# Gate and up products of a split-precision SwiGLU: heads and rests of the tokens in one 512-column matmul

## The chip, the cores and the metric

The kernel runs on one core of one Trainium2 chip. The metric is the device time in microseconds. The kernel before takes 1000.98 us, the median of three runs (1000.97 to 1001.18). All profile rows come from one profiled execution on that core.

## The reference

A trunk of two residual layers over 512 tokens of width 1024, in float32. Layer 0 mixes tokens by causal pooling, layer 1 by dilated window attention. Each layer ends with the block that the change touches:

```python
def swiglu(h, w_gate, w_up, w_down):
    g = jnp.einsum('bsd,df->bsf', h, w_gate)
    u = jnp.einsum('bsd,df->bsf', h, w_up)
    return jnp.einsum('bsf,fd->bsd', jax.nn.silu(g) * u, w_down)

for i in range(DEPTH):            # DEPTH = 2
    h = rmsnorm(x, norm_mix[i])
    x = x + (pool_mixer(h, ...) if i % 2 == 0 else attn_mixer(h, ...))
    h = rmsnorm(x, norm_ffn[i])
    x = x + swiglu(h, w_gate[i], w_up[i], w_down[i])
return rmsnorm(x, norm_final)
```

The hidden width of this block is 2816, which is 22 tiles of 128.

## The kernel before, in words

**Precision.** Every float32 operand is split into a head in the fp32r type and a rest, also fp32r. A product is then three matmuls that accumulate in one PSUM region: weight head by token head, weight head by token rest, weight rest by token head. ACT casts the head (line 139 for weights, line 320 for other tiles) and DVE subtracts it to get the rest (lines 143 and 321).

**Seven products in place of eight.** In groups of two hidden tiles, gate and up are computed by a two-by-two scheme of the Strassen kind: the inner width is cut into halves, the tokens into halves of 256, and sums of weight blocks meet sums of token blocks in seven products, numbered 0 to 6. The token operands (`RIGHT`) are blocks of the normalised tokens `h` or sums of such blocks (`t2`, `t3`, `t4`). The weight sums are made by accumulating DMAs (line 107, on POOL's queue) and by DVE sums (line 145). There are eleven groups per layer, two weight tiles (gate and up) by four inner tiles in each product, so a product has 8 x 3 = 24 matmuls of 256 columns (line 625), each with its own weight load. Seven products use three accumulators, p, r and q: product 0 starts p, 1 starts r, 3 starts q, and 2, 4, 5, 6 add to p or r (`"prpqprp"`). After each product ACT or DVE copies or combines the accumulator into the tile `ct` (`done`, lines 632 to 661); after products 5 and 6 come silu, the gating products, and the sums and splits that make the operands `u_hi` and `u_lo` of the down projection.

**Down.** After groups 3, 6 and 9 a down step (`down`, line 696) multiplies the gated results of three groups by the down weights, again in seven products, each 18 matmuls of 512 columns (line 712) in two token blocks; DVE adds each accumulator into the residual `x` (lines 719 and 721). The last two groups have a plain form (lines 766 to 768).

**Order.** PE runs in the order of the program text; the other engines are ordered by priorities (`URGENT` for accumulator copies after products 0 to 4). Within the feed-forward block, PE's order is `FFN_ORDER`: groups 0 and 1 interleaved, then group by group, each down step as a whole after its group. The weights stand in one queue in the same order. `weights(i)` loads up to ten entries ahead into five raw tiles (`wraw`; three more, `vraw`, for sums), and splits up to four ahead into a ring of five head and rest tiles (`RING`, `wspl`): entry k takes the buffers of entry k - 5. `held` counts entries that an earlier position in the queue still occupies.

**PSUM.** There are eight banks of 512 float32 columns. Four are the rotating pool `mm`, four the feed-forward block's pool `fps` (two for p, two for r). An accumulator of a group is half gate, half up, 256 columns each, in one bank.

Four lines of the product:

```python
for g in range(2):
    for c in range(4):
        for k, (w, xx) in enumerate(((whi, hi), (whi, lo), (wlo, hi))):
            nc.tensor.matmul(ps[:, g, :], lhsT=w[:, g, c, :], rhs=xx[:, c, :], ...)
```

Of the kernel before, what the change touches and what calls it, by code (L numbers as in the profile page):

```python
# [10 lines left out]
F32 = mybir.dt.float32  # L11
# [35 lines left out]
FFN_ORDER = (  # L47
    [("two", 0)] + [("quad", n) for n in (2, 3)] + [("down", 0)]
    + [("quad", n) for n in (4, 5, 6)] + [("down", 1)] + [("quad", n) for n in (7, 8, 9)] + [("down", 2)]
    + [("quad", 10)] + [("last", 3)]  # L50
)

TWO = [(g, i) for g in (0, 1) for i in (0, 3)] + [(g, i) for i in (1, 2, 4, 5, 6) for g in (0, 1)]
# [5 lines left out]
def trunk_kernel(ctx: ExitStack, tc: tile.TileContext, x_in, xT, gam, gains, consts, ident_d, w0, wT, w1, wv, w_down, out):  # L59
# [15 lines left out]
    mm = ctx.enter_context(tc.tile_pool(name="mm", bufs=4, space=bass.MemoryType.PSUM))  # L75
# [92 lines left out]
    def enqueue_ffn(layer):  # L168
# [27 lines left out]
        def down(b):  # L196
            pairs = BLOCKS[b]
            at = layer * (NF // 2) + pairs[0]
            dn[b] = [{}, {}]
            for i in range(7):  # L200
                for js, a, n in zip(dn[b], (at, at + 2), (2, len(pairs) - 2)):
                    operand(js, i, lambda m, k: tiles[k, :, a : a + n, COLS[m]], (n, S), 10)

        for step, n in FFN_ORDER:
            if step == "two":
                for g, i in TWO:
                    quad(n + g, i, 5)
            elif step == "quad":
                for i in range(7):
# [32 lines left out]
    h_both = [stat.tile([P, NC * S + 2 * SHIFT], F32R, name=f"h_{part}") for part in ("hi", "lo")]  # L242

    def tokens_at(shift):
        return [h[:, shift : shift + NC * S].rearrange("p (c s) -> p c s", c=NC) for h in h_both]
# [105 lines left out]
    def out_projection(js, where, hi, lo, norm, shift, four, tps, hook=None):  # L351
# [22 lines left out]
        ws = [weights(js[4 + i], split_ahead=4 + i, load_ahead=6 + i) for i in range(4)]  # L374
        for b in range(4):
# [20 lines left out]
    with ExitStack() as pctx:  # L396
# [137 lines left out]

        third = out_projection(j_out, BY_GROUP, z_hi, z_lo, norm, SHIFT, [mm.tile([P, S], F32, name="mm") for _ in range(4)], turned_banks, lambda: group_products(1, early))

    def ffn(layer, norm, third, nxt):
# [8 lines left out]
        with ExitStack() as fctx:  # L546
# [5 lines left out]
            fps = open_pool("ffps", 2, space=bass.MemoryType.PSUM)  # L552
            early_u = open_pool("ffa", 2)
            third_chain = norm.chain.ins
            h_hi, h_lo = tokens_at(SHIFT)
            block = lambda t, k, n: t[:, 4 * k : 4 * k + 4, HALVES[n]]

# [3 lines left out]
            t2, t3, t4 = ([fp.tile([P, 4, 256], F32R, name=f"t_{part}{i}") for part in ("hi", "lo")] for i in (2, 3, 4))  # L561
            fp.tile([P, SHIFT], F32, name="gap3")
            T_hi, T_lo = ([block(h, 0, 1), t2[i], t3[i], t4[i]] for i, h in enumerate((h_hi, h_lo)))
            RIGHT = (
                [(block(h_hi, 0, 0), block(h_lo, 0, 0))] + [(T_hi[i], T_lo[i]) for i in (0, 1)]
                + [(block(h_hi, 1, 0), block(h_lo, 1, 0)), (T_hi[2], T_lo[2])]
                + [(block(h_hi, 1, 1), block(h_lo, 1, 1)), (T_hi[3], T_lo[3])]
            )
# [12 lines left out]
            class Group:  # L581


                def __init__(self, n, ct):
                    self.n, self.ct, self.sums = n, ct, {}
                    self.lst = ct.rearrange("p m n g c -> p (m n g) c")
                    pool = early_u if n % 4 < 2 else late_u[0]
                    self.u = u_of[n] = [pool.tile([P, 7, 256], F32R, name=t) for t in ("u_hi", "u_lo")]

                def first_half(self):  # L590

                    (hi, lo), lst = self.u, self.lst
# [21 lines left out]
                def product(self, i):  # L614
                    if i == 3:
                        self.sums["q"] = mm.tile([P, S], F32, name="mm").rearrange("p (g c) -> p g c", g=2)
                    elif i < 2:
                        self.sums["pr"[i]] = fps.tile([P, 2, 256], F32, name="pr"[i])
                    ps = self.sums["prpqprp"[i]]
                    whi, wlo = weights(gu[self.n][i])  # L620
                    hi, lo = RIGHT[i]
                    for g in range(2):
                        for c in range(4):
                            for k, (w, xx) in enumerate(((whi, hi), (whi, lo), (wlo, hi))):
                                nc.tensor.matmul(  # L625
                                    ps[:, g, :], lhsT=w[:, g, c, :], rhs=xx[:, c, :],
                                    start=i in (0, 1, 3) and g + c + k == 0, stop=c == 3 and k == 2, skip_group_check=True,
                                )
                    with tc.high_priority(URGENT if i < 5 else 100):
                        self.done(i)  # L630

                def done(self, i):
# [12 lines left out]
                    elif i == 5:  # L645
                        nc.vector.tensor_add(ct[:, 0, 1], r, ct[:, 0, 1])
                        nc.scalar.activation(ct[:, 0, :, 0, :], ct[:, 0, :, 0, :], AF.Silu)
                        nc.vector.tensor_mul(ct[:, 0, :, 0, :], ct[:, 0, :, 0, :], ct[:, 0, :, 1, :])
                        nc.scalar.activation(ct[:, 1, 1, 0, :], ct[:, 1, 1, 0, :], AF.Silu)
                        nc.vector.tensor_mul(ct[:, 1, 1, 0, :], ct[:, 1, 1, 0, :], ct[:, 1, 1, 1, :])  # L650
                        self.first_half()
# [42 lines left out]
            r_tile = lambda: by_four(fps.tile([P, 2, 256], F32, name="r").rearrange("p g c -> p (g c)"))  # L694

            def down(b):

                pairs = BLOCKS[b]

                p, r = ([fps.tile([P, 2, 256], F32, name=t).rearrange("p g c -> p (g c)") for _ in range(2)] for t in "rp")  # L700
                q = [mm.tile([P, S], F32, name="mm") for _ in range(2)]
                where = (0, 1, 2, 3, 6, 5, 4)
                target = ((0, 0, 1), (1, 1, -1), (0, 1, 1), (0, 0, 1), (1, 1, -1), (0, 1, 1), (1, 0, -1))
                for i, acc in enumerate((p, r, p, q, p, r, p)):
                    ws = [weights(js[i], held=z) for z, js in enumerate(dn[b])]
                    half, n, sign = target[i]
                    for t in range(2):
                        for c, pair in enumerate(pairs):
                            whi, wlo = (w[:, c % 2, :] for w in ws[c // 2])
                            hi, lo = (u[:, where[i], t * P : (t + 1) * P] for u in u_of[pair])  # L710
                            for k, (u, w) in enumerate(((hi, whi), (hi, wlo), (lo, whi))):
                                nc.tensor.matmul(  # L712
                                    acc[t], lhsT=u, rhs=w, start=i in (0, 1, 3) and c + k == 0,
# [3 lines left out]
                        with tc.high_priority(URGENT):  # L717
                            if sign > 0:
                                nc.vector.tensor_add(to, acc[t], to)
                            else:  # L720
                                nc.vector.tensor_sub(to, to, acc[t])

            for kind, n in FFN_ORDER[:-1]:
                if kind == "two":
                    groups = [Group(n, ct_common), Group(n + 1, ct_tile(hn, "ct_second"))]
                    with tc.issue_after(third_chain):
                        first_tokens(0, t1r)
                        first_tokens(1, b21r)
                    for at, (g, i) in enumerate(TWO):
                        if at in (0, 2):  # L730
                            b = 2 + at // 2
                            if b == 2:
                                late_banks[b] = third
# [513 lines left out]
```

## Time and profile before

| what | value |
|---|---|
| median of the runs | 1000.98 us |
| profiled execution, first to last instruction (span) | 998.8 us |
| PE busy | 990.8 us, 6575 matmuls |
| PE weight loads busy | 908.1 us |
| DVE busy | 784.4 us |
| ACT busy | 529.1 us |
| granted TensorE clock, mean | 0.999 |

The profile gives no other time for its execution than the span; what lies around it, the median less the span, is 2.2 us. Busy time is the union of an engine's instructions. PE's matmuls overlap in their tails, so a matmul's duration (281 ns for 256 columns) is longer than the distance from one start to the next. Weight loads are listed as PEld and run beside the matmuls. A row of a group reads: line, engine, operation, tiles written and read, shapes, count, then total busy time, mean duration, and the idle time of the engine before them with what ended it. A row of the timeline begins with start and duration.

### The profile page before, as it was taken

How to read it: one execution, taken by the hardware profiler on the slowest of the kernel's cores; microseconds unless marked ns; L12 is line 12 of the kernel's file. 1: busy time of each engine (PE TensorE's matmuls, PEld its weight loads, DVE VectorE, ACT ScalarE, POOL GpSimd, SP SyncE). 2: the span in 40 equal slices, each digit the busy share in tenths (PEclk: the TensorE clock that was granted, in tenths of full speed). 3: DMA queues.
4: the chain of work that ended last, by engine and by line, in shares of the span. 5: the costliest groups of instructions: out<-in, count | busy, mean ns of one | idle time of the engine just before them, and what ended most of it. 6: DMA issues, size and time to landing. Idle time of an engine off the chain costs nothing.

```text
span 998.8 us, 16590 instructions
## 1 busy us (share of the span) xinstructions
PE 990.8 (99%) x6575; PEld 908.1 (91%) x6575; DVE 784.4 (79%) x1116; ACT 529.1 (53%) x838; POOL 113.1 (11%) x114
## 2 busy tenths in 40 slices
PE   9999999999999999999999999999999999999997
PEld 8888999989989998989888899899998998999896
DVE  6475899898888888777887457479989889788875
ACT  5573666545644554573543544356654554455354
POOL 0002010110111100002112023101011101211000
PEclk9999999999999999999999999999999999999999
DMA  9457276668559755524211249527666855975522
GB/s 335 177 168 190 63 197 174 152 189 234 149 128 290 179 137 155 182 71 134 85 56 53 83 141 267 103 61 191 179 159 198 235 148 121 294 176 141 153 66 84
DMA packets 76461, 157.29 MB, mean 157 GB/s; under 512 B 5904, under 2 KB 6288, under 8 KB 76384
## 3 DMA queue, kind: packets, MB, share of 16 engines
q1 hardware_dynamic: 58000, 121.00, 36.2%
q0 software_dynamic: 18096, 34.98, 20.5%
q8 instruction: 51, 0.84, 0.3%
q10 hardware_dynamic: 288, 0.27, 0.1%
q14 instruction: 26, 0.21, 0.1%
HBM read 154.08 MB, written 2.13 MB: 156 GB/s over the span
## 4 chain that ended last, share of the span: by engine, by line
PE 98%; ACT 1%; DVE 0%; issue 0%; ACTq 0%
PE p L625 25%; PE r L625 13%; PE r L712 10%; PE mm L625 6%; PE p L712 5%; PE mm L766 4%; PE mm L227 4%; PE mm L229 4%; PE mm L228 4%; PE mm L712 2%; PE early L443 2%; PE mm L363 2%; PE mm L361 2%; PE mm L362 2%; PE mm L1129 1%; PE tp L955 1%
## 5 line engine op out<-in xcount | busy, mean ns | idle before, releaser
L139 ACT CAST whi<-wraw 128x1024 fp32r<-128x1024 f32 (+2 forms) x189 | 184.8, 981 | 184.3 <-issue 50.8
L143 DVE TENSOR_TENSOR wlo<-wraw,whi 128x1024 fp32r<-128x1024 f32 (+2 forms) x190 | 221.1, 1165 | 74.8 <-ACT whi L139 74.1
L139 ACT CAST whi<-vraw 128x1024 fp32r<-128x1024 f32 (+1 forms) x102 | 99.6, 976 | 144.8 <-DVE vraw L145 53.7
L625 PE MATMUL p<-t_hi,wlo 128*128 128x256 f32 x528 | 149.8, 284 | 0.0
L625 PE MATMUL p<-t_lo,whi 128*128 128x256 f32 x528 | 149.4, 283 | 0.0
L625 PE MATMUL p<-t_hi,whi 128*128 128x256 f32 x528 | 148.4, 281 | 0.0
L143 DVE TENSOR_TENSOR wlo<-vraw,whi 128x1024 fp32r<-128x1024 f32 (+1 forms) x102 | 114.9, 1127 | 13.9 <-ACT whi L139 13.7
L625 PEld LDWEIGHTS p<-t_hi,whi 128*128 128x128 f32 x528 | 100.0, 189 | 0.0
L625 PE MATMUL r<-h_hi,wlo 128*128 128x256 f32 x352 | 99.9, 284 | 0.0
L625 PEld LDWEIGHTS p<-t_hi,wlo 128*128 128x128 f32 x528 | 99.6, 189 | 0.0
L625 PE MATMUL r<-h_lo,whi 128*128 128x256 f32 x352 | 99.6, 283 | 0.0
L625 PEld LDWEIGHTS p<-t_lo,whi 128*128 128x128 f32 x528 | 99.3, 188 | 0.0
L625 PE MATMUL r<-h_hi,whi 128*128 128x256 f32 x352 | 99.0, 281 | 0.0
L145 DVE TENSOR_TENSOR vraw<-vraw,wraw 128x1024 f32<-128x1024 f32 x68 | 76.6, 1127 | 0.8
L107 POOL DMA_DIRECT2D wraw<-w x22 | 26.6, 1211 | 436.1 <-DVE wlo L143 126.2
L625 PEld LDWEIGHTS r<-h_hi,whi 128*128 128x128 f32 x352 | 66.7, 189 | 0.0
L625 PEld LDWEIGHTS r<-h_hi,wlo 128*128 128x128 f32 x352 | 66.4, 189 | 0.0
L625 PEld LDWEIGHTS r<-h_lo,whi 128*128 128x128 f32 x352 | 66.2, 188 | 0.0
L227 PE MATMUL mm<-h_hi,whi 128*128 128x512 f32 (+1 forms) x176 | 64.9, 369 | 0.0
L229 PE MATMUL mm<-h_hi,wlo 128*128 128x512 f32 (+1 forms) x176 | 63.6, 361 | 0.0
L228 PE MATMUL mm<-h_lo,whi 128*128 128x512 f32 (+1 forms) x176 | 63.4, 360 | 0.0
L712 PE MATMUL r<-whi,u_lo 128*128 128x512 f32 x144 | 56.1, 390 | 0.0
(329 smaller groups left out, 2493.2 us busy)
## 6 DMA issues: line engine op xcount, KB each, us to landing
wraw<-w SPq DMA_DIRECT2D x116, 512.0 KB, 4.9
wraw<-w_down SPq DMA_DIRECT2D x32, 512.0 KB, 3.6
vraw<-w SPq DMA_DIRECT2D x22, 512.0 KB, 5.5
wraw<-w POOLq DMA_DIRECT2D x22, 512.0 KB, 7.6
vraw<-w POOLq DMA_DIRECT2D x22, 512.0 KB, 9.0
wraw<-wT SPq DMA_DIRECT2D x16, 512.0 KB, 4.4
wraw<-w_down SPq DMA_DIRECT2D x24, 256.0 KB, 2.6
vraw<-w_down SPq DMA_DIRECT2D x6, 512.0 KB, 5.4
```

The costliest lines, as they stand in the source:

```text
L107: nc.gpsimd.dma_start(dst, more, accum_op=ALU.add)
L139: nc.scalar.copy(hi[:, :n], raw[:, :n])
L143: nc.vector.tensor_sub(lo[:, :n], raw[:, :n], hi[:, :n].bitcast(F32))
L145: nc.vector.tensor_add(raws[into][:, :n], raws[into][:, :n], raws[more][:, :n])
L227: nc.tensor.matmul(ps, lhsT=whi, rhs=xhi, start=first, stop=False, **kw)
L228: nc.tensor.matmul(ps, lhsT=whi, rhs=xlo, start=False, stop=False, **kw)
L229: nc.tensor.matmul(ps, lhsT=wlo, rhs=xhi, start=False, stop=last, **kw)
L361: nc.tensor.matmul(ps, lhsT=xhi, rhs=w[0][:, k, :], start=first, stop=False)
L362: nc.tensor.matmul(ps, lhsT=xhi, rhs=w[1][:, k, :], start=False, stop=False)
L625: nc.tensor.matmul(ps[:, g, :], lhsT=w[:, g, c, :], rhs=xx[:, c, :], start=i in (0, 1, 3) and g + c + k == 0, stop=c == 3 and k == 2, skip ...
L712: nc.tensor.matmul(acc[t], lhsT=u, rhs=w, start=i in (0, 1, 3) and c + k == 0, stop=c == len(pairs) - 1 and k == 2, skip_group_check=True,)
L766: nc.tensor.matmul(ps, lhsT=u, rhs=w[:, m, :], start=z + m + k == 0, stop=z == 1 and m == 1 and k == 2,)
```

## The change

In groups 2 to 9 of each layer (`PAIRED`) a triple of matmuls becomes a pair for products 0, 2, 3, 5 and 6. The token tiles for heads and rests are made as one tile with an extra index z, so one matmul moves the 256 head columns and the 256 rest columns under the weight head, into the two halves of a bank: results with heads go to the first half, results with rests to the second. The weight rest by token head follows as a 256-column matmul into the first half. Products 1 and 4 keep three matmuls of 256 columns, product 1 into a second half, product 4 into a first.

A bank now holds one weight tile, so an accumulator is a pair of banks. A group has three: a (which alternates between two pairs from group to group), q and c. Product 0 starts a, which ACT copies whole into q; product 2 adds to a, and ACT copies a whole into c. Product 3 adds to q, 1 and 5 to c, 4 and 6 to a. When a result leaves its pair, ACT copies the second half into `ct` and DVE adds the first half.

PE's order is written out (`PLAN`): within a group 2, 3, 1, 4, then product 0 of the next group, then 5 and 6. In the queue the weights of 1, 2, 3, 4 stand in that order. Where a down step falls, its product 0 comes ahead of the group's 5 and 6, its products 1 to 5 after them, then the next group's product 0, then its product 6. The down step's accumulators are the free bank pair, q's pair and c's pair. The pool `mm` becomes one tile of four banks, handed out in turn by `Ring`. The tiles `u` are opened when first written.

```diff
-FFN_ORDER = (
-    [("two", 0)] + [("quad", n) for n in (2, 3)] + [("down", 0)]
...
+BODY, USED = (1, 2, 3, 4), (2, 3, 1, 4)
+PAIRED = range(2, 10)
+
+
+def _plan():
+    first = lambda n: [("quad", n, 0)] if n in PAIRED else []
+    steps = TWO[:-1] + first(2) + TWO[-1:]
+    for n in PAIRED:
+        steps += [("quad", n, i) for i in USED]
+        ends = [("quad", n, 5), ("quad", n, 6)]
+        if n % 3 == 0:
+            b = n // 3 - 1
+            steps += [("down", b, 0)] + ends + [("down", b, i) for i in range(1, 6)] + first(n + 1) + [("down", b, 6)]
+        else:
+            steps += first(n + 1) + ends
+    return steps + [("one", 10, i) for i in range(7)] + [("last", 3, 0)]
...
-    mm = ctx.enter_context(tc.tile_pool(name="mm", bufs=4, space=bass.MemoryType.PSUM))
+    mm_banks = ctx.enter_context(tc.tile_pool(name="mm", bufs=1, space=bass.MemoryType.PSUM)).tile([P, 4, S], F32, name="mm")
...
+    mm = Ring(*(mm_banks[:, i, :] for i in range(4)))
...
-        for step, n in FFN_ORDER:
...
+        for kind, n, i in PLAN:
+            if kind == "one":
+                quad(n, i, 5 if n < 2 else 10)
+            elif kind == "quad":
+                if i == USED[0]:
+                    for each in BODY:
+                        quad(n, each)
+                elif i not in BODY:
                     quad(n, i)
-            elif step == "down":
-                down(n)
+            elif kind == "down":
+                down(n, i)
...
-    h_both = [stat.tile([P, NC * S + 2 * SHIFT], F32R, name=f"h_{part}") for part in ("hi", "lo")]
+    h_both = stat.tile([P, 2, NC * S + 2 * SHIFT], F32R, name="h")
...
+            F0, F1 = (fps.tile([P, 2, S], F32, name=f"f{i}") for i in range(2))
+            M0, M1 = mm_banks[:, 0:2, :], mm_banks[:, 2:4, :]
...
-                def product(self, i):
+                def product(self, i, held=0):
+                    whi, wlo = weights(gu[self.n][i], held=held)
+                    right = RIGHT[i]
+                    if self.pairs:
+                        a, q, c = self.pairs
+                        to = (a, c, a, q, a, c, a)[i]
+                        for g in range(2):
+                            for k in range(4):
+                                w, rest, more = whi[:, g, k, :], wlo[:, g, k, :], dict(skip_group_check=True)
+                                if i in (1, 4):
+                                    at = to[:, g, HALVES[i == 1]]
+                                    nc.tensor.matmul(at, lhsT=w, rhs=right[:, 0, k, :], start=False, stop=False, **more)
+                                    nc.tensor.matmul(at, lhsT=w, rhs=right[:, 1, k, :], start=False, stop=False, **more)
+                                else:
+                                    at = to[:, g, HALVES[0]]
+                                    both = to[:, g, :].rearrange("p (z c) -> p z c", z=2)
+                                    nc.tensor.matmul(both, lhsT=w, rhs=right[:, :, k, :], start=i == 0 and k == 0, stop=False, **more)
+                                nc.tensor.matmul(at, lhsT=rest, rhs=right[:, 0, k, :], start=False, stop=k == 3, **more)
+                        with tc.high_priority(URGENT if i < 5 else 100):
+                            self.paired_done(i)
+                        return
...
+                def paired_done(self, i):
+                    ct = self.ct
+                    a, q, c = self.pairs
+                    own, more = HALVES
+                    if i == 0:
+                        nc.scalar.copy(q, a)
+                    elif i == 2:
+                        nc.scalar.copy(c, a)
+                    elif i == 3:
+                        nc.scalar.copy(ct[:, 0, 0], q[:, :, more])
+                        nc.vector.tensor_add(ct[:, 0, 0], q[:, :, own], ct[:, 0, 0])
+                    elif i == 1:
+                        nc.scalar.copy(ct[:, 1, 1], c[:, :, more])
+                    elif i == 4:
+                        nc.vector.scalar_tensor_tensor(
+                            ct[:, 1, 1], a[:, :, own], -1.0, ct[:, 1, 1], op0=ALU.mult, op1=ALU.subtract
+                        )
+                    elif i == 5:
+                        nc.scalar.copy(ct[:, 0, 1], c[:, :, more])
+                        nc.vector.tensor_add(ct[:, 0, 1], c[:, :, own], ct[:, 0, 1])
+                        self.gate_first()
+                    elif i == 6:
+                        nc.scalar.copy(ct[:, 1, 0], a[:, :, more])
+                        nc.vector.scalar_tensor_tensor(
+                            ct[:, 1, 0], a[:, :, own], -1.0, ct[:, 1, 0], op0=ALU.mult, op1=ALU.subtract
+                        )
+                        nc.scalar.activation(ct[:, 1, 0, 0, :], ct[:, 1, 0, 0, :], AF.Silu)
+                        nc.vector.tensor_mul(ct[:, 1, 0, 0, :], ct[:, 1, 0, 0, :], ct[:, 1, 0, 1, :])
+                        self.second_half()
...
+                if kind == "down":
+                    if i == 0:
+                        downs[n] = Down(n, spare_pairs[0], M0, F1)
+                        spare_pairs.reverse()
+                    downs[n].product(i)
+                    continue
+                if i == 0 and kind == "quad":
+                    groups[n] = Group(n, ct_common, (spare_pairs[0], M0, F1))
+                    spare_pairs.reverse()
+                elif n == 10 and i == 0:
+                    groups[n] = Group(n, ct_common)
+                groups[n].product(i, held={1: -2, 2: 1, 3: 1}.get(i, 0) if kind == "quad" else 0)
```

`gate_first`, not shown, holds the silu and gating lines of product 5 that stood in `done`; `Down` holds the matmuls and sums of `down`, one product per call.

More of the change, by code (lines that the diff above doesn't have):

```diff
@@ L615, in product @@
                     if i == 3:
[L616 removed]
+                        self.sums["q"] = by_g(mm.tile())
                     elif i < 2:
[L618 removed]
+                        self.sums["pr"[i]] = by_g((fp_ring, fr_ring)[i].tile())
                     ps = self.sums["prpqprp"[i]]
[L620 removed]
@@ L693, in ffn, with __init__, product @@
             by_four = lambda t: t.rearrange("p (j t) -> p j t", j=4)
[L694 to L705, printed above, removed]
+            r_tile = lambda: by_four(fr_ring.tile())
+            class Down:
+                def __init__(self, b, p, r, q):
+                    self.b, self.accs = b, (p, r, p, q, p, r, p)
+                def product(self, i):
+                    pairs, js = BLOCKS[self.b], dn[self.b]
+                    where = (0, 1, 2, 3, 6, 5, 4)
+                    target = ((0, 0, 1), (1, 1, -1), (0, 1, 1), (0, 0, 1), (1, 1, -1), (0, 1, 1), (1, 0, -1))
+                    ws = [weights(j[i], held=z) for z, j in enumerate(js)]
                     half, n, sign = target[i]
                     for t in range(2):
+                        acc = self.accs[i][:, t, :]
                         for c, pair in enumerate(pairs):
@@ L718, in down @@
                             if sign > 0:
-                                nc.vector.tensor_add(to, acc[t], to)
+                                nc.vector.tensor_add(to, acc, to)
                             else:
[L721 to L733, printed above, removed]
-                                norm.prepare(3, COLS)
-                            else:
-                                late_banks[b] = [r_tile(), by_four(mm.tile([P, S], F32, name="mm"))]
-                                for half in range(2):
-                                    norm.turn(b, half, late_banks[b][half])
-                            late(b, 1)
-                        if at in (4, 6, 8):
-                            for b in (2, 3):
-                                late(b, at // 2)
-                        groups[g].product(i)
@@ new lines, in product @@
+                                nc.vector.tensor_sub(to, to, acc)
+            mm.at = 0
+            groups = {0: Group(0, ct_common), 1: Group(1, ct_tile(hn, "ct_second"))}
+            downs, spare_pairs = {}, [M1, F0]
+            with tc.issue_after(third_chain):
+                first_tokens(0, t1r)
+                first_tokens(1, b21r)
+            for at, (kind, n, i) in enumerate(PLAN[:-1]):
+                if at in (0, 2):
+                    b = 2 + at // 2
+                    if b == 2:
+                        late_banks[b] = third
+                        norm.prepare(3, COLS)
+                    else:
+                        late_banks[b] = [r_tile(), by_four(mm_banks[:, 3, :])]
+                        for half in range(2):
+                            norm.turn(b, half, late_banks[b][half])
+                    late(b, 1)
+                if at in (4, 6, 8):
+                    for b in (2, 3):
+                        late(b, at // 2)
+                if kind == "down":
[10 more added lines that the diff above has]
+                groups[n].product(i, held={1: -2, 2: 1, 3: 1}.get(i, 0) if kind == "quad" else 0)
+                if (n, i) == (1, 6):
@@ L744, in ffn @@
                     held.close()
                     late_u.append(open_pool("ffb", 2))
-                elif kind == "quad":
-                    group = Group(n, ct_common)
-                    for i in range(7):
-                        group.product(i)
-                else:
-                    down(n)
             norm = Norm(nxt, ct_common.rearrange("p m n g c -> p (m n g c)")[:, :D])
```

80 lines of the change are left out of this document (43 added, 37 removed).

## The prediction

> **What bounds the kernel now.** I began with the shares by engine and the chain of waits on the page, then went to PE's own waits.
>
> ```profile
> span 998.8 us, 16590 instructions
> PE 990.8 (99%) x6575; PEld 908.1 (91%) x6575; DVE 784.4 (79%) x1116; ACT 529.1 (53%) x838; POOL 113.1 (11%) x114
> ...
> PE 98%; ACT 1%; DVE 0%; issue 0%; ACTq 0%
> PE p L625 25%; PE r L625 13%; PE r L712 10%; PE mm L625 6%; PE p L712 5%; PE mm L766 4%; PE mm L227 4%; PE mm L229 4%; PE mm L228 4%; PE mm L712 2%; PE early L443 2%; PE mm L363 2%; PE mm L361 2%; PE mm L362 2%; PE mm L1129 1%; PE tp L955 1%
> ```
>
> ```profile
> PE mm L261 <- DVE odd_rows L255: 1.1, 1, 1.1
> PE mm L1129 <- ACT ropea L1115: 0.3, 1, 0.3
> ```
>
> PE is the chain, and it waits 1.4 us in all. L625, the gate and up products, holds 44% of the span. So time is won only by shortening PE's stream, and lost as soon as something makes PE wait. The span lies 2.2 us under the median of 1000.98; I keep those 2.2 us and add to the median.
>
> A busy PE tells nothing of its pace, so I counted starts in stretches with one kind of matmul. First two rows of the groups by shape, for the duration of one (281 and 389 ns), then the stretches: length, PE busy (count), PEld, DVE, ACT, POOL, clock, DMA share, GB/s.
>
> ```profile
> L625 PE MATMUL p<-t_hi,whi 128*128 128x256 f32 x528 | 148.4, 281 | 0.0
> ...
> L712 PE MATMUL r<-whi,u_hi 128*128 128x512 f32 x144 | 56.0, 389 | 0.0
> ```
>
> ```profile
> 158.00:194.00 36.00, 36.00 (x306) 36.00 (x305) 31.61 (x37) 20.92 (x28) 4.48 (x4) 1.00 0.67 161
> 226.00:282.00 56.00, 56.00 (x469) 56.00 (x469) 45.43 (x52) 31.42 (x41) 6.91 (x6) 1.00 0.74 190
> ...
> 375.00:400.00 25.00, 25.00 (x112) 20.70 (x111) 21.62 (x29) 10.32 (x14) 2.00 (x2) 1.00 0.60 160
> ...
> 448.00:452.30 4.30, 4.30 (x38) 4.30 (x37) 4.01 (x9) 3.25 (x7) 0.60 (x1) 1.00 0.76 232
> 201.00:209.40 8.40, 8.40 (x38) 6.94 (x37) 8.40 (x11) 4.35 (x5) 0.00 (x0) 1.00 0.16 38
> ```
>
> A count takes in the matmuls cut by the edges, so the duration of one goes on top of the stretch. Groups 4 to 6 (second row): (56.00 + 0.28) / 469 = 120.0 ns from one 256-column matmul to the next. Groups 2 and 3 (first row): 36.28 / 306 = 118.6 ns, from the same code. The down products of 512 columns (third row): (25.00 + 0.39) / 112 = 226.7 ns. Twice the columns cost 106.7 ns more, so 120.0 - 106.7 = 13.3 ns of each pair of weight load and matmul do not depend on columns. The clock is 1.00 in all these rows.
>
> **The change, part by part.**
>
> *Fewer pairs on PE.* In groups 2 to 9 of both layers, products 0, 2, 3, 5 and 6 issue for each of 8 weight tiles (gate/up by 4) one 512-column and one 256-column matmul in place of three of 256. That is 16 x 5 x 8 = 640 triples, each one load and one matmul fewer, with the same columns. A triple goes from 360.0 to 226.7 + 120.0 = 346.7 ns: 13.3 ns saved in groups 4 to 9, 355.8 - 346.7 = 9.1 in groups 2 and 3. Of the 640, 480 are of the first kind and 160 of the second: 6.4 + 1.5 = **7.8 us off PE's stream**. The trace has no alternation of the two sizes. If the 118.6 rhythm comes back after the change in the 1,408 narrow matmuls left in those groups (640 in triples, 768 in products 1 and 4), up to 1,408 x 1.4 = 2.0 us more are saved; if every triple starts from 118.6, 640 x 9.1 = 5.8. I take 7.8 with 5.8 to 9.8 as ends. A wide product then takes 8 x 346.7 = 2.77 us, a narrow one 24 x 120.0 = 2.88, a group 19.6 in place of 20.2.
>
> The wide matmul reads its columns in two runs, from the heads and from the rests. The nearest row is the fourth above: there the by-halves projection (L227 to L229) reads and writes 256 columns in four runs of 64, at (4.30 + 0.28) / 38 = 120.5 ns. Runs cost nothing there, and I book nothing. [...]
>
> *More copies on ACT and DVE.* Rows by form:
>
> ```profile
> L139 ACT CAST whi<-wraw 128x1024 fp32r<-128x1024 f32 x156 | 163.6, 1051 | 128.7 <-issue 37.3 <-PE p L625 20.5 <-PE mm L228 17.8
> L320 ACT CAST u_hi<-ct 128x1280 fp32r<-128x1280 f32 x16 | 20.3, 1269 | 0.9 <-DVE ct L609 0.3
> L636 ACT COPY keep<-p 128x512 f32<-128x512 f32 x22 | 12.8, 582 | 4.6 <-PE p L625 4.6
> ...
> L653 ACT ACTIVATE ct<-p 128x256 f32<-128x256 f32 x20 | 7.5, 373 | 0.0
> ...
> L143 DVE TENSOR_TENSOR wlo<-wraw,whi 128x1024 fp32r<-128x1024 f32 x156 | 196.7, 1262 | 60.6 <-ACT whi L139 60.0
> L644 DVE SCALAR_TENSOR_TENSOR ct<-p,ct 128x512 f32<-128x512 f32 x20 | 13.7, 687 | 11.4 <-PE p L625 11.4
> L650 DVE TENSOR_TENSOR ct<-ct 128x256 f32<-128x256 f32 x20 | 8.4, 419 | 0.5 <-ACT ct L649 0.5
> L658 DVE SCALAR_TENSOR_TENSOR ct<-p,ct 128x256 f32<-128x256 f32 x20 | 8.4, 418 | 0.0
> ```
>
> Per group, ACT had three copies of 512 columns; it now has four, and two of 1024 from bank to bank. No such copy is in the trace: it lies between 0.58 us (L636) and twice that, 1.16. I take 1.05, the row of the same width (L139). Extra: 0.58 + 2 x 1.05 + 0.04 for the last silu (0.37 to 0.41) = 2.7 us a group. From the second row of windows, ACT had 31.42 / 56 x 20.2 = 11.3 us of work a group, now 14.0 of 19.6, 71%. DVE gains 0.69 - 0.42 + 0.42 = 0.7 us: 45.43 / 56 x 20.2 = 16.4 becomes 17.1 of 19.6, 87%. Neither is a bound by its sum. What counts is where PE waits for them.
>
> *Accumulators.* Before, the accumulators of two groups in a row lay in different banks, and PE waited for none. Now a group has pair a (two of them alternate between groups), q and c. Product 2 may write a only after the copy to q has read it: products 5 and 6 of the group before lie between (5.5 us) or, where a down step ends, its product 6 (18 x 226.7 = 4.1 us), against 1.05 us of copy. Product 0's interleaving is this cover; without it the copy would cost PE about 1.2 us in each of 16 groups, 19 us. Product 1 writes c only after the copy to c, which starts when product 2 ends: product 3 alone covers it, 2.77 us. It needs the matmul's tail (0.28 - 0.12 = 0.16), at worst one ACT instruction already running (1.27, L320) and 1.05: 2.5 us. **0.25 us to spare**, so I book 0 and keep the miss as a rival. The copy to c also waits until DVE has read c after product 5 of the group before; while it stands at ACT's head, the casts of the next weights queue behind it, which have two products of lead or more (next part).
>
> *Weights.* The split buffers stay a ring of five in the order of the queue, but product 1 is used third. Product 5's weights need product 1's buffer, and products 4 and next-0 lie between: the lead falls from four products (11.5 us) to two (5.65), against 1.05 + 1.26 us for the split. Covered. The loads on SP keep their bytes; the raw tile of product 0 is held three places longer, of five. Splits waited for such loads only this much:
>
> ```profile
> ACT whi L139 <- DMA wraw<-w: 2.1, 6, 0.7
> ```
>
> *The down steps.* These are the tight places, one after groups 3, 6 and 9 of each layer, six in all. The trace of the first, at product 3 of the down step:
>
> ```profile
> 202.95 1.48 DVE L321 TENSOR_TENSOR u_lo<-ct,u_hi 128x1280 fp32r<-128x1280 f32 x1
> 204.35 0.68 DVE L721 TENSOR_TENSOR x<-x,p 128x512 f32<-128x512 f32 x1
> 204.95 1.22 DVE L145 TENSOR_TENSOR vraw<-vraw,wraw 128x1024 f32<-128x1024 f32 x1
> 206.08 0.68 DVE L719 TENSOR_TENSOR x<-r,x 128x512 f32<-128x512 f32 x1
> 206.69 0.68 DVE L143 TENSOR_TENSOR wlo<-wraw,whi 128x512 fp32r<-128x512 f32 x1
> ```
>
> ```profile
> 207.59 0.39 PE L712 MATMUL mm<-whi,u_hi 128*128 128x512 f32 x1
> ...
> 209.18 0.39 PE L712 MATMUL mm<-wlo,u_hi 128*128 128x512 f32 x1
> ```
>
> DVE is busy without a break (8.40 of 8.40 in the last window row), and ends the weights at 207.37 that PE reads at 209.18: 1.8 us to spare. The change puts down product 0 ahead of the group's products 5 and 6, so from the end of product 5 to this read PE takes 4.1 us less. DVE's work in between loses that product's two sums into x (0.60 each from start to start, 206.08 to 206.69) and gains 0.7: the spare becomes 1.8 - 4.1 + 1.2 - 0.7 = -1.8 if nothing is done earlier. But by the ring of five, the second weights of down 1 and the first of down 2 now get their buffers when down 0 ends, a whole product before product 5 ends. One split of 512, its sum and one split of 1024 (0.6 + 0.6 + 1.1 us, as spaced in these rows) move out: +0.5. So a stall between 0 and 1.8 us at each, 0 to 11 us over six. Nearer to the second figure, since those buffers are free by then, I book 0.3 each: **+2 us**.
>
> Sum: 1000.98 - 7.8 + 2 = **995.2**, a span of about 993.0.
>
> **The rivals.**
>
> *A, the c copy is late (slower).* If ACT's order puts one weight cast more ahead of it, it ends 1.05 - 0.25 = 0.8 us late and PE stands before product 1 in each of 16 groups: 12.8 us, 1000.98 - 7.8 + 12.8 = 1006. It decides against the change from 7.8 / 16 = 0.49 us a group. For it: casts wait for PE at the head of ACT's queue (37.3 and 20.5 us in L139's row) and ACT rises to 71%. Against: the copies have the high priority and the cast's buffer is mostly long free.
>
> *B, the down steps take the gain.* 1.2 us at each of six, 7 us: 1000. For it: DVE without a break there. Against: the buffers that come free earlier.
>
> *C, no gain per pair.* The 13.3 ns turn out to go with columns or with a change of size, or the wide matmul is slowed by its two runs: 1001 and the 2 us of the down steps, 1003 at most. Two sizes of the trace and the by-halves row speak against it. That the wide matmul is issued as two has the same answer. [...]
>
> *D, no wait at all and the 118.6 rhythm throughout:* 1000.98 - 9.8 = 991.2.
>
> **How the numbers follow.** Forecast (992 to 998.5) 0.62, D 0.07, B 0.13, C 0.05, A 0.13. About 0.2%, 2 us, can be told from no change. Faster, under 999.0: 0.62 + 0.07 + 0.02 of B = 0.71. Slower, over 1003: A and 0.01 of C = 0.14. The same: 0.15. The range leaves out A beyond 1002.5 and some of D: 991.5 to 1002.5. The likeliest alone: 992 to 998.5.
>
> **What would show it.** PE should have 640 matmuls fewer than 6,575, about 5,935, and a wide product in groups 4 to 9 should take 2.77 us. The bank copies of 1024 columns should take 1.05 us, and PE should wait for none of them. A wait of PE named after the copy to c is A; one after a weight rest at L143 in the down steps is B; wide products over 2.85 us without a wait are C. The forecast is wrong if the waits are absent and the span stays above 996, or if PE's waits sum to over 6 us.

## The result, and the profile after

The changed kernel takes **1247.72 us**, the kernel before 1001.08 us in the same comparison: a ratio of 1.2463, 95% interval 1.2445 to 1.2480. The forecast was 995.2 us, and its range ended at 1002.5. The first profiled execution of the change was disturbed (2696.9 us), so the profile shown here is that of a second profiling of the same kernel, whose runs have a median of 1245.76 us (ratio 1.2450, 1.2431 to 1.2468) and whose profiled execution spans 1242.8 us.

From its page: the span, busy time by engine, and the rows of 40 slices for PE and for the granted clock.

```profile
span 1242.8 us, 15421 instructions
...
PE 1052.3 (85%) x5935; PEld 889.5 (72%) x5935; DVE 804.6 (65%) x1132; ACT 566.2 (46%) x886; POOL 113.8 (9%) x114
...
PE   9778989879979988886787897897897898799795
...
PEclk9899999999999999997988998999999999999999
```

PE issues 5,935 matmuls, as the prediction said, and yet is busy for 1052.3 us where it was busy for 990.8. And it stands still for 1242.8 - 1052.3 = 190.5 us, where it stood for 8.0. So of 244 us more span, 182.5 are idle time of PE and 61.5 are the same or less work that takes longer. The idle time lies all over the kernel, also in slices 2 to 4, whose products the change did not touch.

PE's waits in this kernel, the largest rows (what PE wrote, its line, who released it; us in total, times, longest):

```profile
PE mm L800 <- DVE x L809: 31.8, 30, 1.6
PE mm L800 <- DVE x L807: 19.5, 20, 1.7
PE mm L250 <- DVE ropea L954: 13.0, 9, 5.6
PE mm L250 <- DVE e L999: 12.6, 3, 4.6
PE mm L664 <- ACT f L691: 12.2, 6, 2.3
PE mm L860 <- DVE x L376: 9.9, 13, 0.8
PE mm L250 <- DVE u_lo L499: 8.4, 2, 6.7
...
PE f L800 <- DVE x L807: 6.5, 6, 1.1
```

Before, two rows with 1.4 us stood here. Now PE waits for DVE and ACT in every kind of stage where they read accumulators: in the down products (L800; the readers L807 and L809 are the sums into `x`) and their plain form for the last groups (L860), in the projections of the token mixers (L250, untouched by the change), in the gate and up products (L664; L691 is the copy of a into c). Seven of these eight rows write `mm`, one writes `f`.

One down product shows what PE waits for. Product 4 of a down step writes one bank of a pair for token block 0 and then the other for token block 1, 9 matmuls each; product 5 follows at 263.86. PE's timeline (start, duration, what it wrote and read, the wait in brackets), and DVE's:

```profile
257.34 0.39 PE L800 MATMUL mm<-whi,u_hi 128*128 128x512 f32 x1
...
259.16 0.39 PE L800 MATMUL mm<-whi,u_lo 128*128 128x512 f32 x1
260.65 0.50 PE L800 MATMUL mm<-whi,u_hi 128*128 128x512 f32 x1 [1.11 <-DVE x L809]
260.99 0.39 PE L800 MATMUL mm<-wlo,u_hi 128*128 128x512 f32 x1
...
263.86 0.47 PE L800 MATMUL mm<-whi,u_hi 128*128 128x512 f32 x1 [0.87 <-DVE x L809]
```

```profile
259.91 0.68 DVE L809 TENSOR_TENSOR x<-x,mm 128x512 f32<-128x512 f32 x1
```

Token block 0 is done with the matmul of 259.16. DVE reads its bank from 259.91 to 260.59, and only then, at 260.65, does PE begin block 1, which goes into the **other bank** of the pair and needs nothing from that read. What the two banks share is the tile: `mm` is one tile of four banks now. The wait is listed with 1.11 us but costs more: from the last matmul ahead of it to the second one behind it go 1.83 us (259.16 to 260.99) where two steps of 0.227 are 0.45. That is a loss of 1.38 us, 0.27 more than listed.

### The profile page after: what moved, and what is told of

It reads as the page before. It is cut to its first block, busy times and chain, and to the rows that moved or that the text cites. A ratio compares the mean times of both kernels' runs of the same rounds, so it can differ in the third digit from the quotient of the medians.

```text
span 2696.9 us, 15421 instructions
## 1 busy us (share of the span) xinstructions
PE 2553.0 (95%) x5935; PEld 1841.7 (68%) x5935; DVE 819.6 (30%) x1132; ACT 570.9 (21%) x886; POOL 113.8 (4%) x114
## 5 line engine op out<-in xcount | busy, mean ns | idle before, releaser
L800 PE MATMUL mm<-whi,u_hi 128*128 128x512 f32 x216 | 177.4, 821 | 44.7 <-DVE x L809 24.5
L800 PE MATMUL mm<-whi,u_lo 128*128 128x512 f32 x216 | 179.1, 829 | 0.0
L800 PE MATMUL mm<-wlo,u_hi 128*128 128x512 f32 x216 | 178.4, 826 | 0.0
L665 PE MATMUL f<-h,wlo 128*128 128x256 f32 x336 | 177.9, 529 | 0.0
L664 PE MATMUL f<-h,whi 128*128 128x512 f32 x208 | 172.4, 836 | 0.0
L800 PEld LDWEIGHTS mm<-whi,u_hi 128*128 128x128 f32 x216 | 70.5, 326 | 142.6 <-issue 58.7
L664 PE MATMUL mm<-h,whi 128*128 128x512 f32 x176 | 145.9, 836 | 10.9 <-ACT f L691 10.9
L250 PE MATMUL mm<-h,whi 128*128 128x512 f32 (+1 forms) x176 | 133.4, 758 | 21.0 <-DVE ropea L954 10.0
L664 PE MATMUL f<-t,whi 128*128 128x512 f32 x160 | 131.6, 829 | 0.0
L252 PE MATMUL mm<-h,wlo 128*128 128x512 f32 (+1 forms) x176 | 131.5, 747 | 0.0
L251 PE MATMUL mm<-h,whi 128*128 128x512 f32 (+1 forms) x176 | 130.3, 740 | 0.0
L677 PEld LDWEIGHTS f<-h,whi 128*128 128x128 f32 x288 | 105.5, 434 | 5.5 <-DVE ct L736 2.2
L664 PEld LDWEIGHTS f<-h,whi 128*128 128x128 f32 x208 | 77.1, 371 | 45.5 <-issue 44.6
```

The lines of the kernel that those rows point to most:

```text
L250: nc.tensor.matmul(ps, lhsT=whi, rhs=xhi, start=first, stop=False, **kw)
L251: nc.tensor.matmul(ps, lhsT=whi, rhs=xlo, start=False, stop=False, **kw)
L252: nc.tensor.matmul(ps, lhsT=wlo, rhs=xhi, start=False, stop=last, **kw)
L664: nc.tensor.matmul(both, lhsT=w, rhs=right[:, :, k, :], start=i == 0 and k == 0, stop=False, **more)
L665: nc.tensor.matmul(at, lhsT=rest, rhs=right[:, 0, k, :], start=False, stop=k == 3, **more)
L677: nc.tensor.matmul(ps[:, g, :], lhsT=w[:, g, c, :], rhs=right[:, z, c, :], start=i in (0, 1, 3) and g + c + k == 0, stop=c == 3 and k == 2 ...
```

## The experiments

Theory after the result, **waits by tile**: the program makes a write of PE wait for the readers of the whole tile, so a tile of several banks ties each bank to the readers of the others. Rivals: the wide matmul with its two runs is slow (C of the prediction); the copies from bank to bank come late (A); the new order makes the waits.

**Is it the wide matmul?** The changed kernel once more, and with each 512-column matmul of the pairs issued as two of 256:

```diff
-both = to[:, g, :].rearrange("p (z c) -> p z c", z=2)
-nc.tensor.matmul(both, lhsT=w, rhs=right[:, :, k, :], start=i == 0 and k == 0, stop=False, **more)
+nc.tensor.matmul(at, lhsT=w, rhs=right[:, 0, k, :], start=i == 0 and k == 0, stop=False, **more)
+nc.tensor.matmul(to[:, g, HALVES[1]], lhsT=w, rhs=right[:, 1, k, :], start=False, stop=False, **more)
```

> The changed kernel as it is, for a profile at its time of about 1247 us. Theory 1, waits: PE stands still at the accumulators or the weights in each of the 16 paired groups; PE's waits then sum to some 250 us, the pace of a 512-column matmul stays near 227 ns and that of a 256-column one near 120. Theory 2, pace: PE hardly waits (under 20 us) and every matmul in the whole kernel, the pooling and attention stages too, starts later after the one before: 227 ns becomes about 283, 120 about 150. Theory 3, the chip and not the kernel: on this chip the time is about 995 us.

> The changed kernel with each 512-column matmul of the pairs cut into two of 256 columns into the same two halves of the bank; order, accumulators, copies and tiles as changed. Theory 1, waits: the order and the accumulators are the cause, so the time stays near 1247 us (up to 8 us more). Theory 2, pace: if the wide matmul lowers the pace, the time falls to about 1003 us; if something in the program that is not the wide matmul lowers it, it stays near 1247. Theory 3: about 1003 us, as the changed kernel with 8 us more on PE.

Measured: 1245.76 us, and 1246.37 (ratio to before 1.2441, 1.2415 to 1.2467). PE's waits in the first sum to about 183 us and not to 250; the rest of the loss is longer busy time. Taking the wide matmuls out again changes nothing that can be told. They are not the loss.

**Is it the tile?** The kernel before, with one edit: the pool of four rotating one-bank tiles becomes the change's one tile of four banks, handed out in turn. Order, products, copies and `fps` stay.

```diff
-mm = ctx.enter_context(tc.tile_pool(name="mm", bufs=4, space=bass.MemoryType.PSUM))
+mm_banks = ctx.enter_context(tc.tile_pool(name="mm", bufs=1, space=bass.MemoryType.PSUM)).tile([P, 4, S], F32, name="mm")
...
+mm = Ring(*(mm_banks[:, i, :] for i in range(4)))
```

> The kernel before, with one edit: the four banks of the pool mm are one tile handed out in turn, as in the change. Theory one-tile: a write of PE into one bank of a tile waits until ACT and DVE have read the other banks of that tile, so each product waits for the reading of the product before it. Then the stages that use mm (pooling, query/key projections, output projections, last down step) lose what they lose in the changed kernel, about 113 us by the waits at these lines there, and the time is 1100 to 1130 us. Rival, order and accumulators: the waits come from the written-out order and the bank-to-bank copies, which this kernel does not have; then about 1001 us.

Measured: **1133.42 us**, ratio 1.1324 (1.1303 to 1.1345), 3.4 us above the upper end expected. Its page and PE's waits:

```profile
span 1132.1 us, 16579 instructions
...
PE 1031.1 (91%) x6575; PEld 923.0 (82%) x6575; DVE 790.0 (70%) x1116; ACT 531.6 (47%) x838; POOL 113.7 (10%) x114
```

```profile
PE mm L237 <- DVE ropea L870: 13.0, 9, 5.6
PE mm L237 <- DVE e L915: 12.6, 3, 4.6
...
PE mm L237 <- DVE u_lo L481: 8.5, 2, 6.8
```

The rows of the changed kernel at L250 come back here at L237 almost to the tenth (13.0, 12.6, and 8.5 for 8.4), with none of its new arithmetic. How a tile is declared is worth 132.6 us in a kernel that is otherwise the one before. That a pool of four tiles became one tile of four banks is therefore a cause, not a companion.

**Does the change gain without it?** The change, with eight tiles of one bank each. A copy or sum over a pair of banks is then two instructions, one for each bank:

```diff
-mm_banks = ctx.enter_context(tc.tile_pool(name="mm", bufs=1, space=bass.MemoryType.PSUM)).tile([P, 4, S], F32, name="mm")
+mm_pool = ctx.enter_context(tc.tile_pool(name="mm", bufs=1, space=bass.MemoryType.PSUM))
+mm_banks = [mm_pool.tile([P, S], F32, name=f"mm{i}") for i in range(4)]
...
-F0, F1 = (fps.tile([P, 2, S], F32, name=f"f{i}") for i in range(2))
+F0, F1 = ([fps.tile([P, S], F32, name=f"f{i}{t}") for t in range(2)] for i in range(2))
...
-    nc.scalar.copy(q, a)
+    for g in range(2):
+        nc.scalar.copy(q[g], a[g])
```

> The changed kernel with eight tiles of one bank each in place of tiles of four and two banks; the readings of a pair are cut into one instruction per bank (on DVE 256 columns twice at 0.42 us for 512 at 0.69, on ACT 0.41 twice for 0.58). Wide matmuls, order, accumulators and weights as in the change. Theory one-tile: PE's waits fall from about 170 us to a few, and the time is what the prediction's sum gave, 993 to 998 us. Rival, order and accumulators: PE keeps its waits at the copies and in the down steps, and the time stays over 1100 us.

> The kernel with eight tiles, and each 512-column matmul of the pairs cut into two of 256. Measures the wide matmul by itself: by the prediction's 13.3 ns a pair (9.1 in groups 2 and 3) this kernel is 640 pairs, 7.8 us, slower than the one with wide matmuls, about 1001 to 1006 us. If the fixed part does not go with the pair, the two are equal.

Measured: **995.79 us**, ratio 0.9949 (0.9937 to 0.9962): 0.5% faster than before, and 0.6 us from the forecast. With the wide matmuls cut in two again: 1001.37, ratio 1.0006 (0.9997 to 1.0015). So the order, the pairs of banks and the copies cost nothing that can be told by themselves (-0.3 to 1.5 us), and the wide matmul is worth 5.6 us. The page of the kernel with one-bank tiles, and all of PE's waits in it:

```profile
span 994.2 us, 15591 instructions
...
PE 985.7 (99%) x5935; PEld 874.5 (88%) x5935; DVE 798.7 (80%) x1196; ACT 572.7 (58%) x982; POOL 113.0 (11%) x114
```

```profile
PE mm L289 <- DVE odd_rows L283: 1.1, 1, 1.1
PE mm L1227 <- ACT ropea L1213: 0.3, 1, 0.3
PE early L472 <- ACT h L447: 0.2, 1, 0.2
PE early L472 <- DVE h L448: 0.2, 1, 0.2
```

190.5 us of idle PE have become 8.5. The tiles of tokens in SBUF, which the change also joined (`h` and `t` for heads and rests), cost no wait worth naming.

**Which tile costs what?** That run changed two things, the tiles and the cut of the copies. Two kernels put one shared tile back each, with the copies still cut by bank:

```diff
-F0, F1 = ([fps.tile([P, S], F32, name=f"f{i}{t}") for t in range(2)] for i in range(2))
+F0, F1 = ([t[:, 0, :], t[:, 1, :]] for t in [fps.tile([P, 2, S], F32, name=f"f{i}") for i in range(2)])
```

```diff
-mm_banks = [mm_pool.tile([P, S], F32, name=f"mm{i}") for i in range(4)]
+mm_tile = mm_pool.tile([P, 4, S], F32, name="mm")
+mm_banks = [mm_tile[:, i, :] for i in range(4)]
```

> The kernel with eight one-bank tiles (995.8 us), with one difference: the two bank pairs F0 and F1 are two-bank tiles again; the four banks of mm stay tiles of their own and the copies stay cut by bank. Theory (PE's write waits until the readers of all banks of the tile are done): the waits on the tiles f come back and no others. In the changed kernel, PE's waits that name f add up to about 20 us (6.5 and 6.2 the largest rows), and what stood in their shadow comes on top: 1015 to 1055 us, no wait outside the feed-forward block. Rival (the eight tiles were fast because their copies are cut by bank, and the size of the tiles does not matter): 996 us, waits of PE under 3 us.

> The kernel with eight one-bank tiles (995.8 us), with one difference: the four banks of mm are one tile again; F0 and F1 stay four tiles and the copies stay cut by bank. Theory (waits by tile): the 133 us that the kernel before lost to the same edit come back outside the groups, and inside the feed-forward block the waits of the down products and of the products into q and a on mm: 1150 to 1220 us. Rival (the cut copies decide): 996 us in the groups, so about 996 + 133 = 1129 us at most.

Measured: 1030.82 us with F0 and F1 as pairs (ratio 1.0297, 1.0283 to 1.0312), 1231.17 us with `mm` as one tile (1.2298, 1.2280 to 1.2317). The cut of the copies is not what helps. PE's waits, first with the pairs, then with the one tile:

```profile
PE f L804 <- DVE x L811: 6.5, 6, 1.7
PE f L345 <- DVE h L349: 5.5, 3, 2.1
```

```profile
PE mm L805 <- DVE x L814: 33.7, 30, 1.6
...
PE mm L252 <- DVE ropea L959: 13.0, 9, 5.6
```

Each tile brings back the waits that carry its name and no others of any size. The pairs alone cost 35 us, the tile of four banks 235 us, 11 us more than the upper end I had expected. The two do not add up (270 against 250 for both, in the changed kernel). A wait that one tile enforces may hide part of the other's, but the changed kernel also has its copies uncut, and no run separates the two.

**What is the interleaving worth?** The prediction priced product 0's early place, ahead of the products 5 and 6 of the group before, as the cover of the copy from a to q: 1.2 us in each of 16 groups. The kernel with one-bank tiles in plain order, where also each down step runs as a whole behind its group:

```diff
-steps += [("quad", n, i) for i in USED]
+steps += first(n) + [("quad", n, i) for i in USED]
...
-steps += [("down", b, 0)] + ends + [("down", b, i) for i in range(1, 6)] + first(n + 1) + [("down", b, 6)]
+steps += ends + [("down", b, i) for i in range(7)]
...
-steps += first(n + 1) + ends
+steps += ends
```

> The kernel with eight one-bank tiles (995.8 us) with the groups no longer interleaved: product 0 goes ahead of its own group's products 2, 3, 1, 4, 5, 6, and each down step runs as a whole after its group. Between product 0 and product 2, which adds to the same accumulator, nothing is left. Theory 1 (the prediction's price, about 1.2 us for the uncovered copy in each of 16 groups): 995.8 + 19 = 1015 us, with waits of PE on the copy from a to q. Theory 2 (with one-bank tiles the first bank is copied while PE still fills the second, 8 matmuls or 1.4 us, and the second bank while PE is in the first one of product 2): no wait, 994.5 to 997.5 us; the two down stalls of the sum would go too.

Measured: 1003.82 us, ratio 1.0032 (1.0020 to 1.0045), so 8.0 us slower than interleaved: neither 19 nor nothing. No wait of PE names the down line L804. The waits behind the copy from a to q, one of them in PE's timeline, and ACT's timeline there:

```profile
PE f L665 <- ACT mm L691: 2.0, 9, 0.5
PE mm L665 <- ACT mm L691: 1.2, 4, 0.4
```

```profile
227.27 0.28 PE L666 MATMUL f<-h,wlo 128*128 128x256 f32 x1
228.05 0.50 PE L665 MATMUL f<-t,whi 128*128 128x512 f32 x1 [0.50 <-ACT mm L691]
228.39 0.27 PE L666 MATMUL f<-t,wlo 128*128 128x256 f32 x1
```

```profile
226.46 1.05 ACT L163 CAST whi<-wraw 128x1024 fp32r<-128x1024 f32 x1 [0.55 <-DMA wraw<-w]
227.41 1.06 ACT L691 COPY mm<-f 128x512 f32<-128x512 f32 x2
```

Here the first bank's copy could have begun while PE filled the second, but a weight cast that started at 226.46 stood ahead of it on ACT: rival A's mechanism, in a kernel without the cover. From 227.27 to 228.39 PE took 1.12 us where a step of 0.12 and one of 0.23 are 0.35, so it lost 0.77 us at this place, again 0.27 more than listed. The 13 waits that are listed make 3.2 us; with 0.27 more for each they come to 6.7, an estimate from these two places, and the rest of the 8.0 us I did not assign.

**Why 5.6 us and not 7.8?** In the kernel with one-bank tiles, five wide products in a row run from the first row's start to the second's, 40 pairs of a 512-column and a 256-column matmul:

```profile
258.25 0.39 PE L665 MATMUL f<-h,whi 128*128 128x512 f32 x1
...
272.28 0.28 PE L660 MATMUL f<-h,whi 128*128 128x256 f32 x1
```

(272.28 - 258.25) / 40 = 350.8 ns a pair, where 226.7 + 120.0 = 346.7 were booked. Two suspects: the two runs of the wide operand, and the change of size at each step. The first was tried with the sum tiles `t` laid out so that head and rest columns adjoin, the second with all wide matmuls of a bank (of a product) ahead of the narrow ones:

```diff
-t_both = [fp.tile([P, 2, 4, 256], F32R, name=f"t{i}") for i in (2, 3, 4)]
+t_both = [fp.tile([P, 4, 2, 256], F32R, name=f"t{i}").rearrange("p k z c -> p z k c") for i in (2, 3, 4)]
```

```diff
+steps = [(g, k, z) for g in range(2) for k in range(4) for z in range(2)]
+if i not in (1, 4):
+    steps.sort(key=lambda s: (s[0], s[2], s[1]))
```

Here z is 0 for the wide matmul and 1 for the narrow one. This is the order in fours, per bank; in eights the key is `(s[2], s[0], s[1])`, the whole product.

> The kernel with eight one-bank tiles (995.8 us), with the three sum tiles t laid out so that the 256 head columns and the 256 rest columns of an inner tile stand next to each other: the wide matmul of products 2 and 6 reads one run of 512 columns; products 0, 3 and 5 read two runs as before. In the kernel with one-bank tiles a wide matmul is followed by the narrow one after 230.6 ns on average with h and with t, where 226.7 were booked. Theory (the second run costs the 4 ns): 227 ns for t, 230.6 for h, 256 x 4 = 1 us faster, 994.8 us. Rival (the change of size costs it, or the weight load): 230.6 ns for both, 995.8 us.

> The kernel with one-bank tiles (995.8 us), with another order inside products 0, 2, 3, 5 and 6: per bank first the four matmuls of 512 columns, then the four of 256, in place of one of each in turn. Now a wide matmul is followed by the next one after 230.6 ns on average where a stretch of 512 columns alone goes at 227. Theory (a change of size costs these 4 ns): three of four wide ones lose it, 480 x 4 ns = 1.9 us, 993.9 us, and 227 ns from wide to wide. Rival (the wide matmul costs it in any order): 995.8 us and 230 ns from wide to wide.

> As the run with fours, but all eight wide matmuls of a product first, over both banks, then the eight narrow ones. Theory (a change of size costs 4 ns): seven of eight lose it, 560 x 4 ns = 2.2 us, 993.6 us. Rival: 995.8 us. In either case the first bank is finished 1.4 us later than in turn, so the copy into c could now come late before product 1; a wait of PE there would show it.

Measured: 995.98 us for the joined tiles (ratio 0.9950, 0.9938 to 0.9963), 995.73 for fours (0.9952, 0.9938 to 0.9965), 996.93 for eights (0.9964, 0.9952 to 0.9977). Against 995.79 that is no gain that can be told from any of them. With the joined tiles, product 2 (read from `t` in one run) and product 3 (read from `h` in two) stand side by side:

```profile
265.84 0.40 PE L665 MATMUL f<-t,whi 128*128 128x512 f32 x1
...
268.65 0.39 PE L665 MATMUL mm<-h,whi 128*128 128x512 f32 x1
...
271.46 0.28 PE L660 MATMUL f<-h,whi 128*128 128x256 f32 x1
```

2.81 us each, 351 ns a pair: the second run costs nothing. In fours, the same five wide products run from here to here:

```profile
257.79 1.10 PE L668 MATMUL f<-h,whi 128*128 128x512 f32 x4
258.72 0.63 PE L662 MATMUL f<-h,wlo 128*128 128x256 f32 x4
259.19 1.10 PE L668 MATMUL f<-h,whi 128*128 128x512 f32 x4
...
271.83 0.28 PE L664 MATMUL f<-h,whi 128*128 128x256 f32 x1
```

14.04 us, again 351.0 ns a pair, although six of a product's eight wide matmuls are now followed by another wide one, so the change of size is not it either. The first rows say where the time goes: four wide matmuls take 0.93 us (257.79 to 258.72), 232 ns each, and four narrow ones 0.47, 118 each. The wide matmul of these products is slow behind another wide one too, as the rival in the expectation of fours had it. Why it takes longer here than the 226.7 ns of a 512-column matmul in the down products stays open. No version was measurably faster than the one with one-bank tiles in the order of the change.

## Why the prediction was wrong

**The step that failed is the part on accumulators**, with the edit that it did not price. The prediction said: "Before, the accumulators of two groups in a row lay in different banks, and PE waited for none", and then followed a, q and c bank by bank. It asked which bank is written while which is read, and found covers for each. The program asks which *tile*. Before, every accumulator was a tile of its own, and that was the cover which made PE's 1.4 us of waits; the change took it away in two edits (`mm` as one tile of four banks, F0 and F1 as tiles of two), and I booked the first at nothing without even naming it as a step. By the runs it costs 132.6 us in the kernel before and 235 us in the kernel with one-bank tiles; F0 and F1 cost 35 there. In the kernel with one-bank tiles readers work in one bank while PE writes another: DVE reads a bank of `mm` from 208.87 to 209.55 us while PE's matmuls into `f` go on, 0.22 to 0.23 us from start to start, and PE's waits are 1.8 us with all readers at work. The tile of four banks is coarser than that.

The prediction had a sign for this case, "if PE's waits sum to over 6 us" the forecast is wrong, and it fired. It had no rival for it: A came nearest in kind (PE stands before a write until a reader is through), but at one place per group for 12.8 us, and B, C and D end at 1003 us at most. In A, one reading was wrong too: of the two waits in L139's row that it puts down to PE, the 37.3 us stand under "issue", and PE's are 20.5 and 17.8.

With that step repaired, the others can be read in the kernel with one-bank tiles:

- *Fewer pairs, -7.8 us.* The count was right (5,935). The size was not: 350.8 ns a pair in place of 346.7. A triple went from 360.0 (or 355.8) to 350.8, so 480 x 9.2 + 160 x 5.0 = 5.2 us, and cutting the wide matmuls again cost 5.6 measured. That is just under the lower end of 5.8. The step took the pace of a 512-column stretch of the down products for that of a mixed one.
- *The runs of the wide operand, nothing.* Right, by the joined tiles, for what a matmul reads: 2.81 us for the product that reads one run and for the one that reads two. The wide matmul writes its bank in one run, so the joined tiles do not test writes in several; for those the prediction's row of four runs, 120.5 ns against 120.0, is the one figure here.
- *Copies.* Booked at 1.05 us, they take 1.00, as the groups by shape of the changed kernel show (here the copy to q):

```profile
L689 ACT COPY mm<-f 128x1024 f32<-128x1024 f32 x10 | 10.0, 1002 | 9.7 <-PE f L665 9.7
```

- *The copy to c, 0.25 us to spare.* With one-bank tiles PE never waits for it, since the first bank is copied (268.32 to 268.90 us in one group) while PE fills the second (from 268.07). That gain was not foreseen in the prediction. How the 0.25 us would have held with whole-pair copies and separate tiles wasn't tried; in the kernels here such copies have the pair in one tile.
- *The interleaving as a cover, 19 us without it.* 8.0 measured, with the down steps put back as well: it was needed, at less than half the price.
- *Weights two products ahead.* Covered: no wait of PE names a weight tile.
- *Down steps, +2 us.* Nothing. No wait of PE names the down line L804. The rest that PE reads first at 209.56 in product 3 of the first down step is the one that DVE has written by 206.34 (DVE's row, then PE's):

```profile
205.66 0.68 DVE L167 TENSOR_TENSOR wlo<-wraw,whi 128x512 fp32r<-128x512 f32 x1
```

```profile
209.56 0.39 PE L804 MATMUL f<-wlo,u_hi 128*128 128x512 f32 x1
```

  So 3.2 us are to spare where I feared a stall of up to 1.8. The prediction gave 0.5 us to the buffers that come free earlier; how much of the difference is theirs no run separates.

So the forecast's 995.2 and the 995.8 of the repaired kernel agree partly by chance: -7.8 + 2 stood for -5.2 + 0.

## What to carry to other kernels

In these runs the waits were made by what the program declares: a buffer that was joined for one wide instruction tied together the readers and writers of its parts (132.6 us for `mm` in the kernel before; 235 us for `mm` and 35 us for F0 and F1 in the kernel with one-bank tiles), also in stages that nobody meant to change. So price the declaration of a tile as an edit of its own. If the profile of before shows an engine that waits for nothing, ask which declarations make that so, and check each against the diff. Where a wide copy has its two banks in one tile, two copies of one bank each were the better bargain here: 160 instructions more on ACT and DVE (982 and 1196 for 886 and 1132), off the bounding engine, against 250 us.

## What the runs showed of the hardware

The clock. In the changed kernel PE stands for 6.66 us in the first layer's mixer, and what follows is slow (PE's timeline, then a window of it and the next: length, PE, PEld, DVE, ACT, POOL, clock, DMA share, GB/s):

```profile
33.14 0.39 PE L252 MATMUL mm<-whi,h 128*128 128x512 f32 x1
40.19 0.80 PE L250 MATMUL mm<-whi,h 128*128 128x512 f32 x1 [6.66 <-DVE u_lo L499]
40.78 0.63 PE L251 MATMUL mm<-wlo,h 128*128 128x512 f32 x1
41.21 0.63 PE L252 MATMUL mm<-whi,h 128*128 128x512 f32 x1
```

```profile
40.20:43.80 3.60, 3.60 (x9) 2.83 (x10) 0.00 (x0) 0.00 (x0) 0.00 (x0) 0.50 0.00 0
44.00:47.00 3.00, 3.00 (x14) 2.47 (x14) 0.00 (x0) 0.00 (x0) 0.00 (x0) 0.99 0.00 0
```

The granted clock is 0.50 for 3.6 us, and 512-column matmuls start 0.43 us apart in place of 0.23. So this wait costs PE its own length and, at half speed for 3.6 us, 1.8 us more.

Shorter waits did the same, but not each time:

```profile
408.91 0.50 PE L664 MATMUL mm<-h,whi 128*128 128x512 f32 x1 [1.98 <-ACT f L691]
```

```profile
409.20:412.60 3.40, 3.40 (x12) 2.87 (x12) 2.04 (x6) 1.78 (x3) 0.00 (x0) 0.51 0.86 196
```

This wait is one of the six in the row of L664 and L691 above, one of 2.25 us and five of 1.98. Two of them, here and near 1003 us, were followed by half the clock; behind the other four it stayed at 1.00. So a wait of 1.98 us was followed by half the clock here, and by the full clock elsewhere.

The mean clock fell from 0.999 to 0.974 in this kernel. Its trace has twelve such stretches, of 3.4 or 6.8 us, before the last matmuls; PE is busy for 48.2 us of them, so some 24 of the 61.5 us of longer busy time are the clock's. The kernel has 152 waits, and 0.27 us beyond each listed one would be 41 us. Both are estimates, and together they come near 61.5 plus the 5.2 us that the pairs save.

The second thing is the 351 ns of a wide and a narrow matmul, in turn or in fours. The excess goes with the wide one (232 ns in fours against 226.7 in the down products), and neither of the two suspects explains it.
